# First loads in another order, weights in quarters, GpSimd left out of the front, and a scheduler with other durations

## The chip, the cores and the metric

The kernel runs on one core of one Trainium2 chip. The metric is the device time of one execution in microseconds, as the median of several runs. Beside the runs stands one execution that the hardware profiler recorded; every row shown here is from that one. Engines have the names of the profile: PE is TensorE's matmul, PEld its weight load, DVE is VectorE, ACT is ScalarE, POOL is GpSimd, SP issues the DMAs.

## What is computed

A decoder trunk of two layers on 512 tokens of width 2048, with 16 learned tokens in front (528 columns in all). Only the first step and the first products of layer 0 matter to the change; the rest is here so that the work behind them can be seen.

```
h = concat(meta_tokens, x)                 # 528 x 2048
h = layer_norm(h, ln_in_g, ln_in_b)
for l in range(2):
    proj = h @ w_in[l]                     # 2048 -> 5120, split in nine parts
    c = c_val * sigmoid(c_glu)             # convolution branch: 31 taps, norm, silu, product
    att = sliding_window_attention(q, k, v, sinks)
    r = rg_lru(causal_conv(r_x))           # recurrent branch
    mixed = concat(c', att', r') @ w_out[l]   # 2048 -> 2048, each branch gated by silu
    h = layer_norm(alpha * h + mixed, ln_post_g[l], ln_post_b[l])
return h[16:]
```

## The kernel before

Data lies with features on the partitions and the 528 tokens in columns. Each float32 product is made of three float32r matmuls: weights and activations are split into a high part (a copy that rounds to float32r) and a low part (the subtraction of it), and `mm3` sums high by high, high by low and low by high. The products of one tile of 128 output features run over 16 blocks of 128 input features.

**The front.** Five tiles of x (four of 128 tokens and one of 16, 2048 wide, loaded in four chunks of 512) come in as rows of tokens (`x_load`). `x_norm` takes statistics of each chunk on VectorE, the root on ScalarE and the reciprocal on VectorE, and scales the four chunks. `turn` transposes one block of 128 features on TensorE into PSUM, brings it out with the gains applied (ScalarE, to `e`), copies it to float32r (VectorE, the cast) and subtracts (GpSimd for three blocks in four, VectorE for the fourth). Phase 0 of the first products covers tiles 0 and 1 (256 columns), phase 1 tiles 2 to 4 (272 columns). In `gemms` the first three output tiles (glu 0, val 0, glu 1) run together, block by block, so that each block of h is used by nine matmuls of a phase as soon as `turn` has it: 144 matmuls in phase 0 and 144 in phase 1. From then on one output tile follows another, both halves of the columns at once.

**Weights.** `weight_load` brings pieces of 128 x 1024 (512 KB) into a ring of two raw buffers (`NRAW`); `weight_split` makes high parts on ScalarE and low parts on VectorE, 512 columns at a time, and frees the raw buffer. The first pieces are the first halves of three tiles, then their second halves.

**The order of the work.** Nothing is ordered by the hardware alone: `Sched` is a planner that runs while the program is built. Every thread (`k.spawn(prio, ...)`) yields one operation at a time with an engine and a reckoned duration; `run` takes the operation that could start first by its own clock, and of equals the one with the lower number. The program of each engine is the order that comes out, and each engine then keeps to it. SP's queue is one more engine ("Q") for the planner. Units ("u") are 78 buffers of one tile that weights, h and temporary results share; `Alloc` takes them by the planner's clock.

The reckoned durations that the change touches are in `mm`, `dma` and `_head`:

```
c = max(n / 2400, self._size(w) / 1200) + 0.003
return self._op("Q", max(0.45, n / 360e3), o, i, ..., 2.0)
kind = next((c for c in r.kinds if len(self.slots[c]) > (0 if r.weight or c != "u" else max(0, 10 - 2 * self.wheld))), None)
```

## Time and profile before

| what | value |
|---|---|
| median of 3 runs | 1490.77 us (1488.93 to 1490.9) |
| the profiled execution | 1489.76 us |
| its span, from first to last instruction | 1488.0 us |
| PE busy | 1451.8 us (98%) |
| VectorE busy | 1049.1 us (71%) |
| ScalarE busy | 706.3 us (47%) |
| GpSimd busy | 20.3 us (1%) |
| loaded and stored | 142.32 MB, mean 96 GB/s |

The profiled execution's own time is 1.76 us over its span and 1.01 us under the median of the runs. A share of busy time is an average over stages with other limits; PE is counted as busy from the start of a matmul to its modelled end, and matmuls overlap, so that short waits between them do not show in the 98%.

### The profile page before, as it was taken

The page shows a single profiled execution, that of the slowest core. Times are in us where ns is not written, and L with a number is a line of the kernel's source. Part 1 is how long each engine was busy: PE and PEld are TensorE (multiplying, and loading weights), DVE is VectorE, ACT ScalarE, POOL GpSimd, SP SyncE. Part 2 cuts the span into 40 slices and gives each one's busy share as a digit, 9 for nine tenths or more (in the row PEclk, how much of TensorE's full clock was granted, in tenths as well). Part 3 has the DMA queues.
Part 4 walks back from the last instruction along what each step waited for, and adds up shares of the span by engine and source line. Part 5 has one row for each costly group of instructions (what it writes and reads, how often), then busy time and mean ns, then how long its engine had stood idle before and what let it go on. Part 6 is the DMA issues. An engine that isn't in the chain of part 4 may idle for free.

```text
span 1488.0 us, 25171 instructions
## 1 busy us (share of the span) xinstructions
PE 1451.8 (98%) x10028; PEld 1350.8 (91%) x10028; DVE 1049.1 (71%) x2111; ACT 706.3 (47%) x1539; POOL 20.3 (1%) x28
## 2 busy tenths in 40 slices
PE   4999999999999999999999999999999999999996
PEld 3999999999999999999999997998788888888885
DVE  7798999984588443354688889999747864434437
ACT  5412458883377332222368134778735853323221
POOL 2200000000000000000000000000000000000000
PEclk9999999999999999999999999999999999999999
DMA  6312522243221223232433033223232222523323
GB/s 231 93 57 85 143 86 65 62 138 106 80 72 58 85 86 114 72 100 85 132 111 93 29 107 120 79 61 118 88 103 86 71 72 90 163 88 114 100 71 113
DMA packets 56549, 142.32 MB, mean 96 GB/s; under 512 B 12464, under 2 KB 20912, under 8 KB 56432
## 3 DMA queue, kind: packets, MB, share of 16 engines
q1 hardware_dynamic: 56432, 140.73, 30.8%
q8 instruction: 78, 1.28, 0.4%
q14 instruction: 39, 0.32, 0.1%
HBM read 128.12 MB, written 4.19 MB: 89 GB/s over the span
## 4 chain that ended last, share of the span: by engine, by line
PE 88%; DVE 7%; ACT 2%; DMA 1%; issue 1%; SPq 0%; DVEq 0%; ACTq 0%
PE p L184 68%; PE b L184 18%; DVE u L160 5%; PE b L188 2%; DVE a L160 2%; ACT u L174 1%; DMA w<-in_win 1%; DVE s L160 0%; DMA a<-in_x 0%; DVE t L160 0%; ACT t L174 0%; DVE P L160 0%; DMA u<-u 0%; SPq L194 0%; PE p L188 0%
## 5 line engine op out<-in xcount | busy, mean ns | idle before, releaser
L184 PE MATMUL p<-u,u 128*128 128x264 f32 (+3 forms) x7824 | 1181.4, 306 | 4.1 <-DVE u L160 2.9
L184 PEld LDWEIGHTS p<-u,u 128*128 128x128 f32 x7824 | 1064.5, 189 | 61.8 <-DVE u L160 4.6
L160 DVE TENSOR_TENSOR u<-w,u 128x512 fp32r<-128x512 f32 x456 | 306.0, 689 | 174.0 <-ACT u L174 170.6
L174 ACT ACTIVATE u<-w 128x512 fp32r<-128x512 f32 x456 | 273.0, 622 | 241.8 <-DMA w<-in_wout 124.3
L184 PE MATMUL b<-u,u 128*128 128x512 f32 (+6 forms) x1568 | 290.5, 324 | 4.3 <-DVE u L160 3.2
L184 PEld LDWEIGHTS b<-u,u 128*128 128x128 f32 (+2 forms) x1568 | 241.4, 185 | 33.9 <-DVE u L160 4.6
L160 DVE SCALAR_TENSOR_TENSOR a<-u,dp,a 128x527 f32<-128x527 f32 (+14 forms) x240 | 179.7, 749 | 4.2
L174 ACT ACTIVATE P<-P,s 100x257 f32<-100x257 f32 (+5 forms) x240 | 111.2, 479 | 28.7 <-DVE s L160 28.7
L160 DVE TENSOR_TENSOR u<-u,u 128x528 f32<-128x528 f32 (+5 forms) x146 | 100.8, 697 | 20.8 <-ACT u L174 17.9
L174 ACT ACTIVATE u<-p 128x528 f32<-128x528 f32 (+2 forms) x71 | 42.4, 598 | 149.0 <-PE p L184 148.8
L174 ACT ACTIVATE u<-u 64x528 fp32r<-64x528 f32 (+5 forms) x112 | 63.8, 584 | 81.0 <-DVE u L160 74.9
L160 DVE SCALAR_TENSOR_TENSOR u<-u,p 128x528 f32<-128x528 f32 (+3 forms) x45 | 30.7, 683 | 68.7 <-ACT u L174 50.6
L174 ACT ACTIVATE t<-b 128x400 fp32r<-128x400 f32 (+3 forms) x112 | 57.1, 510 | 44.0 <-PE b L184 22.0
L160 DVE CUSTOM_DVE_ANT_0 P<-b,con,nsink 100x256 f32<-100x256 f32 (+2 forms) x160 | 67.1, 450 | 3.1 <-PE b L184 2.2
L160 DVE TENSOR_TENSOR t<-b,t 128x400 fp32r<-128x400 f32 (+2 forms) x72 | 41.7, 579 | 13.4 <-ACT t L174 13.0
L184 PE MATMUL b<-t,u 128*128 128x400 f32 (+2 forms) x144 | 50.5, 351 | 0.0
L188 PE MATMUL b<-con,P 100*128 100x100 f32 (+2 forms) x320 | 44.1, 253 | 0.0
L174 ACT ACTIVATE u<-b 128x256 fp32r<-128x256 f32 (+4 forms) x28 | 11.8, 443 | 57.7 <-PE b L188 51.1
L188 PEld LDWEIGHTS b<-con,P 100*128 100x128 f32 (+2 forms) x320 | 35.9, 140 | 3.1 <-DVE s L160 0.4
L160 DVE TENSOR_SCALAR P<-P,s 100x256 f32<-100x256 f32 (+3 forms) x88 | 31.5, 363 | 0.7
L160 DVE SCALAR_TENSOR_TENSOR u<-u,u 128x528 f32<-128x528 f32 (+1 forms) x40 | 27.5, 699 | 5.2 <-ACT u L174 4.7
L174 ACT ACTIVATION_READ_ACCUMULATOR P<-P,s 100x1 f32 (+2 forms) x160 | 30.2, 189 | 0.0
(103 smaller groups left out, 656.7 us busy)
## 6 DMA issues: line engine op xcount, KB each, us to landing
w<-in_win SPq DMA_DIRECT2D x160, 512.0 KB, 3.7
w<-in_wout SPq DMA_DIRECT2D x64, 512.0 KB, 4.1
u<-u SPq DMA_DIRECT2D x48, 120.0 KB, 2.2
a<-in_x SPq DMA_DIRECT2D x8, 256.0 KB, 5.1
P<-in_x SPq DMA_DIRECT2D x8, 256.0 KB, 6.0
u<-u SPq DMA_DIRECT2D x16, 128.0 KB, 2.1
w<-in_pw SPq DMA_DIRECT2D x8, 256.0 KB, 2.6
out<-a SPq DMA_DIRECT2D x8, 256.0 KB, 2.3
```

The source lines that it names most:

```text
L160: return self._op("V", c, outs, ins, lambda: f(**kw))
L174: op = self._op("S", c, outs, ins, lambda: f(**kw))
L184: return self._op("T", c, [out], [w, x], lambda: f(out, w, x, start=start, stop=stop))
L188: return self._op("T", max(2 * self._size(ident) / 2400, 0.11) + 0.005, [out], [x, ident], lambda: f(out, x, ident))
```

## The change

It does these things, all of them in the planning program; what is computed stays the same.

- Loads: after x tile 0 comes the identity (now a tile of its own), then x tile 1 in two halves of 512 KB, then the gains and shifts of the first norm as a small tile of their own (`gin`). The first three weights come in quarters of 128 x 512 (256 KB) into units instead of the two raw buffers. `XBEFORE` and `WBEFORE` set the order: six quarters, tile 2, three quarters, tile 3, three quarters, tile 4, then the parameters and the constants.
- GpSimd has no work left in `turn`; the subtractions are VectorE's.
- A thread may yield a pair of operations; `_head` takes the one that would end first by the reckoned times, with 0.6 us added for VectorE. Scaling of chunks, the eviction in `turn`, the cast and the high parts of the early weights are such pairs of ScalarE and VectorE.
- `x_turn` starts the blocks of a chunk when that chunk is scaled in all tiles of the phase, not when whole tiles are. Low parts of the early weights wait until the first chunk of tile 1 is scaled (`go`). Four threads split the quarters, each with its own number.
- Durations: 0.445 ns a column and 4.5 ns for a matmul, 400 GB/s and 2.65 us of latency for a load.
- Evictions of PSUM (`E`) may take units down to four free ones instead of up to ten; `take_rx` frees the PSUM of the recurrent branch ahead of the wait in `recur`. The same edit from `U()` to `E()` in `values`, `conv_point` and `gate` is left out below.

```diff
+XBEFORE = (2, 2, 3, 4)
+WBEFORE = (0, 0, 6, 9, 12)
...
-    def __init__(self, kinds, dt=F32, w=L, weight=False):
-        self.kinds, self.dt, self.w, self.weight = kinds, dt, w, weight
+    def __init__(self, kinds, dt=F32, w=L, weight=False, keep=10):
+        self.kinds, self.dt, self.w, self.weight, self.keep = kinds, dt, w, weight, keep
...
-        self.free["Q"] = 0.8
+        self.free["Q"] = 0.75
...
-        c = max(n / 2400, self._size(w) / 1200) + 0.003
+        c = max(0.445e-3 * n, self._size(w) / 1200) + 0.0045
...
-        return self._op("Q", max(0.45, n / 360e3), o, i, lambda: f(out=out, in_=in_), 2.0)
+        return self._op("Q", max(0.45, n / 400e3), o, i, lambda: f(out=out, in_=in_), 2.65)
...
+            if isinstance(r, tuple):
+                return min(r, key=lambda o: self._start(o) + o.cost + (0.6 if o.eng == "V" else 0.0))
...
-                kind = next((c for c in r.kinds if len(self.slots[c]) > (0 if r.weight or c != "u" else max(0, 10 - 2 * self.wheld))), None)
+                kind = next((c for c in r.kinds if len(self.slots[c]) > (0 if r.weight or c != "u" else max(0, r.keep - 2 * self.wheld))), None)
...
-    con = cp.tile([128, NCONST], F32, name="con")
-    k.fixed = {par.tensor.name, con.tensor.name}
-    ident = con[:, C_ID:C_ID + 128]
+    con = cp.tile([128, C_ID], F32, name="con")
+    ident = cp.tile([128, 128], F32, name="ident")
+    gin = cp.tile([128, 32], F32, name="gin")
+    k.fixed = {par.tensor.name, con.tensor.name, gin.tensor.name, ident.tensor.name}
...
+    def E(keep=4):
+        return Alloc("u", F32, L, False, keep)
...
-    pieces = [(w, i) for i in range(2) for w in stream[0:NGROUP[0]]]
-    pieces += [(w, i) for w in stream[NGROUP[0]:] for i in range(-(-w.src.shape[1] // 1024))]
-    flow = dict(ahead=AHEAD, held=0, loaded=0)
+    pieces = [(w, 512 * i, 512) for i in range(4) for w in stream[0:NGROUP[0]]]
+    early = len(pieces)
+    pieces += [(w, i, min(1024, w.src.shape[1] - i)) for w in stream[NGROUP[0]:] for i in range(0, w.src.shape[1], 1024)]
+    flow = dict(ahead=AHEAD, held=0, loaded=0, x=0, split=0, go=False)
...
-        for w, i in pieces:
-            m = min(1024, w.src.shape[1] - 1024 * i)
-            raw = yield Alloc("w")
-            yield k.dma(raw[:, 0:m], w.src[:, 1024 * i:1024 * i + m])
-            w.raw.append((raw, m))
+        for n, (w, c, m) in enumerate(pieces):
+            if n < early:
+                yield Until(lambda: flow["x"] >= XBEFORE[n // NGROUP[0]])
+                raw = yield U(F32, 512)
+            else:
+                raw = yield Alloc("w")
+            yield k.dma(raw[:, 0:m], w.src[:, c:c + m])
+            w.raw.append((c, raw))
...
-    def weight_split():
-        for w, i in pieces:
-            yield Until(lambda: len(w.raw) > i)
-            raw, m = w.raw[i]
+    def weight_split(which):
+        for n in which:
+            w, c, m = pieces[n]
+            yield Until(lambda: w.raw and w.raw[-1][0] >= c and flow["split"] == n)
+            raw = next(r for o, r in w.raw if o == c)
...
-                yield S(out=wh, in_=r, func=AF.Copy)
+                a = S(out=wh, in_=r, func=AF.Copy)
+                yield (a, V("tensor_copy", out=wh, in_=r)) if n < early else a
+                yield Until(lambda: flow["go"])
...
+            flow["split"] += 1
...
-    xtok, xown = [None] * 5, [None] * 5
+    xtok, xown = [[None] * 4 for _ in range(5)], [None] * 5
...
-            own = []
+            yield Until(lambda: flow["loaded"] >= WBEFORE[i])
...
-                xt = [big[:, c, 0:512] for c in range(4)]
+                big = big.rearrange("p a c -> p (a c)")
+                xt = [big[:, 512 * c:512 * c + 512] for c in range(4)]
...
+                own = []
...
-            for c in range(4):
-                op = k.dma(xt[c][0:rows], t["x"][i * 128:i * 128 + rows, c * 512:(c + 1) * 512])
-                op.outs = [f"x{i}{c}"]
+            step = 2 if i == 1 else 1
+            for c in range(0, 4, step):
+                out = big[:, 512 * c:512 * (c + step)] if i < 2 else xt[c][0:rows]
+                op = k.dma(out, t["x"][i * 128:i * 128 + rows, c * 512:(c + step) * 512])
+                op.outs = [f"x{i}{c + s}" for s in range(step)]
+                if i == 1:
+                    op.lat += 1.0
...
-            k.spawn((0.8 if i < 2 else 1.42) + 0.01 * i, x_norm(i, xt, own))
-            if i == 4:
-                yield Until(lambda: flow["loaded"] >= 6)
-                yield k.dma(con[:, 0:C_ID], t["con"][:, 0:C_ID])
+            k.spawn((0.8 if i < 2 else 1.8) + 0.01 * i, x_norm(i, xt, own))
+            if i == 0:
+                yield k.dma(ident, t["con"][:, C_ID:NCONST])
...
-                yield k.dma(con[:, C_ID:NCONST], t["con"][:, C_ID:NCONST])
-                yield k.dma(par, t["par"])
-            if i in (1, 2):
-                yield Until(lambda: flow["loaded"] >= i)
+                yield k.dma(gin, t["par"][:, P_G0:P_G0 + 32])
+            flow["x"] = i + 1
+        yield k.dma(par, t["par"])
+        yield k.dma(con, t["con"][:, 0:C_ID])
...
+        def scale(c):
+            x = xt[c][0:rows]
+            ops = (V("tensor_scalar", out=x, in0=x, scalar1=mv[0:rows, 0:1], scalar2=mv[0:rows, 1:2], op0=ALU.subtract, op1=ALU.mult),
+                   S(out=x, in_=x, func=AF.Identity, scale=mv[0:rows, 1:2], bias=mv[0:rows, 2:3]))
+            for op in ops:
+                op.outs = [f"x{i}{c}"]
+                op.ins = [f"x{i}{c}", mv.tensor.name]
+            yield ops if c else ops[0]
+            xtok[i][c] = xt[c]
+        yield from scale(0)
+        if i == 1:
+            flow["go"] = True
...
-        for c, x in enumerate(xt):
-            x = x[0:rows]
-            if i > 1 or c > 2:
-                yield V("tensor_scalar", out=x, in0=x, scalar1=mv[0:rows, 1:2], scalar2=mv[0:rows, 2:3], op0=ALU.mult, op1=ALU.add)
-            else:
-                yield S(out=x, in_=x, func=AF.Identity, scale=mv[:, 1:2], bias=mv[:, 2:3])
+        for c in range(1, 4):
+            k.spawn((1.38 if i < 2 else 1.8) + 0.1 * c, scale(c))
+        yield Until(lambda: xtok[i][3] is not None and xtok[i][1] is not None and xtok[i][2] is not None)
...
-        xtok[i] = xt
...
-            for i in tiles:
-                yield Until(lambda: xtok[i] is not None)
...
-                k.spawn(1.4 + 0.2 * f, turn(f, d, tiles))
+                yield Until(lambda: all(xtok[i][d // 4] is not None for i in tiles))
+                k.spawn(1.85 if f else 1.4 + 0.1 * (d // 4), turn(f, d, tiles))
...
-            yield k.tr(ps[:, o:o + ROWS[i]], xtok[i][d // 4][0:ROWS[i], cs], ident[0:ROWS[i], 0:ROWS[i]])
+            op = k.tr(ps[:, o:o + ROWS[i]], xtok[i][d // 4][0:ROWS[i], cs], ident[0:ROWS[i], 0:ROWS[i]])
+            op.ins = [f"x{i}{d // 4}", ident.tensor.name] + ([x.tensor.name for x in xown[i]] if d == KT - 1 else [])
+            yield op
...
-        g, bb = par[:, P_G0 + d:P_G0 + d + 1], par[:, P_G0 + 16 + d:P_G0 + 17 + d]
+        g, bb = gin[:, d:d + 1], gin[:, 16 + d:17 + d]
...
-        yield S(out=e[:, 0:n], in_=ps[:, 0:n], func=AF.Identity, scale=g, bias=bb)
+        yield (S(out=e[:, 0:n], in_=ps[:, 0:n], func=AF.Identity, scale=g, bias=bb),
+               V("tensor_scalar", out=e[:, 0:n], in0=ps[:, 0:n], scalar1=g, scalar2=bb, op0=ALU.mult, op1=ALU.add))
...
-        yield V("tensor_copy", out=hi[:, c0:c0 + n], in_=e[:, 0:n])
-        yield (G if d % 4 < 3 else V)("tensor_tensor", out=lo[:, c0:c0 + n], in0=e[:, 0:n], in1=hi[:, c0:c0 + n].bitcast(F32), op=ALU.subtract)
+        yield (V("tensor_copy", out=hi[:, c0:c0 + n], in_=e[:, 0:n]), S(out=hi[:, c0:c0 + n], in_=e[:, 0:n], func=AF.Copy))
+        yield V("tensor_tensor", out=lo[:, c0:c0 + n], in0=e[:, 0:n], in1=hi[:, c0:c0 + n].bitcast(F32), op=ALU.subtract)
...
-        e = yield U()
+        e = yield E()
...
-        c = yield U()
+        c = yield E()
...
-        x = yield U()
-        s = yield U()
+        x = yield E()
...
+        s = yield U()
...
-    def recur(y, j, pr):
-        l, d = y.l, dp[y.l]
-        x = yield U()
+    def take_rx(y, j, pr):
+        x = yield E()
...
+        k.spawn(7, recur(y, j, x))
+    def recur(y, j, x):
+        l, d = y.l, dp[y.l]
...
-            k.spawn(2 if fn is not recur else 7, fn(y, i, pr))
+            k.spawn(2, fn(y, i, pr))
...
-        todo += [(recur, j, FULL) for j in range(4)]
+        todo += [(take_rx, j, FULL) for j in range(4)]
...
-        k.spawn(1, weight_split())
+        for q in range(4):
+            k.spawn(1.35 + 0.1 * q, weight_split(range(q * NGROUP[0], (q + 1) * NGROUP[0])))
+        k.spawn(1, weight_split(range(early, len(pieces))))
...

```

## Rows read from the trace of the kernel before

**Rows 1.** Costliest groups on PE, 76 to 1480 us: busy, mean | idle before.

```profile
L184 PE MATMUL p<-u,u 128*128 128x264 f32 (+1 forms) x7629 | 1145.6, 305 | 2.5 <-DVE u L160 1.6 <-ACT u L174 0.7
L184 PE MATMUL b<-u,u 128*128 128x264 f32 (+4 forms) x1472 | 272.0, 326 | 2.2 <-DVE u L160 1.2 <-ACT u L174 0.9
```

**Rows 2.** Chain that ended last, 0 to 90 us: start, length, what.

```profile
5.57 6.38 DMA w<-in_win
...
34.68 0.35 PE b L184 x3
...
35.74 0.36 PE b L184 x3
...
47.06 0.91 PE b L188 x6
...
51.10 0.38 PE b L188 x3
...
75.33 14.72 PE p L184 x119
```

**Rows 3.** Timeline of PE, 64 to 67 us: start, length, instructions.

```profile
64.73 0.93 PE L184 MATMUL p<-u,u 128*128 128x272 f32 x6
...
65.87 0.90 PE L184 MATMUL p<-u,u 128*128 128x272 f32 x6
```

**Rows 4.** Timeline of all engines, 9 to 19 us, from the second x tile on.

```profile
10.05 1.40 DVE L160 BATCH_NORM_STATS2 s<-a 128x6 f32<-128x512 f32 x2
...
11.04 0.69 PE L188 MATMUL b<-con,a 128*128 128x128 f32 x2 [11.04 <-ACT a L174]
...
11.48 0.26 DVE L160 BATCH_NORM_AGGREGATE s<-s 128x2 f32<-128x24 f32 x1
11.78 0.29 ACT L174 ACTIVATE s<-s,cst 128x1 f32<-128x1 f32 x1
...
12.11 0.16 DVE L160 RECIPROCAL s<-s 128x1 f32<-128x1 f32 x1 [0.36 <-ACT s L174]
...
15.84 0.54 ACT L174 ACTIVATE t<-b,par 128x256 f32<-128x256 f32 x1
...
18.45 0.58 PE L184 MATMUL p<-u,u 128*128 128x256 f32 x1 [1.32 <-DVE u L160]
```

**Rows 5.** Groups on VectorE and GpSimd, 10 to 62 us, each shape apart.

```profile
L160 DVE CAST u<-t 128x272 fp32r<-128x272 f32 x16 | 9.1, 571 | 4.8 <-ACT t L174 4.6
L160 DVE CAST u<-t 128x256 fp32r<-128x256 f32 x16 | 5.3, 353 | 0.9 <-ACT t L174 0.9
...
L160 DVE TENSOR_TENSOR u<-t,u 128x256 fp32r<-128x256 f32 x4 | 1.7, 413 | 0.0
...
L167 POOL TENSOR_TENSOR u<-t,u 128x256 fp32r<-128x256 f32 x12 | 10.4, 884 | 23.5 <-DVE u L160 23.5
L167 POOL TENSOR_TENSOR u<-t,u 128x272 fp32r<-128x272 f32 x12 | 9.7, 813 | 18.3 <-DVE u L160 18.3
```

**Rows 6.** Groups on ScalarE, 4 to 62 us, each shape apart.

```profile
L174 ACT ACTIVATE u<-w 128x512 fp32r<-128x512 f32 x16 | 9.8, 622 | 4.6 <-DMA w<-in_win 4.6
...
L174 ACT ACTIVATE t<-b,par 128x256 f32<-128x256 f32 x16 | 8.7, 559 | 5.7 <-PE b L188 5.5 <-POOL u L167 0.2
```

**Rows 7.** One line on VectorE, 19 to 62 us: duration ns min/median/max.

```profile
L160 DVE CAST u<-t x31: 270/302/869, 19.7 to 61.7; 128x272 fp32r<-128x272 f32 x16, 128x256 fp32r<-128x256 f32 x15
L160 DVE TENSOR_TENSOR u<-w,u x13: 657/679/1230, 19.0 to 61.0; 128x512 fp32r<-128x512 f32 x13
L160 DVE TENSOR_SCALAR P<-P,s x8: 521/535/973, 25.0 to 43.1; 128x512 f32<-128x512 f32 x8
```

**Rows 8.** Stretches: busy us of PE, PEld, DVE, ACT, POOL; clock; DMA; GB/s.

```profile
10.00:15.00 5.00, 1.38 (x4) 0.58 (x4) 3.44 (x10) 4.74 (x8) 0.00 (x0) 1.00 1.04 404
...
25.00:30.00 5.00, 2.88 (x13) 2.24 (x14) 5.00 (x11) 2.78 (x6) 2.70 (x3) 0.69 0.01 2
30.00:35.00 5.00, 5.00 (x31) 5.00 (x30) 4.14 (x11) 3.25 (x6) 2.84 (x3) 0.63 0.73 203
```

More of the change, by code (lines that the diff above doesn't have):

```diff
@@ L637, in conv_point @@
     def conv_point(y, j, pr):
-        o = yield U()
+        o = yield E()
         for pv, ov in pr.views(o):
@@ L684, in values @@
     def values(y, p, pr):
-        x = yield U()
-        m = yield U()
+        x = yield E()
         for pv, xv in pr.views(x):
@@ L689, in values @@
         pr.free()
+        m = yield U()
         mv = m[:, 0:384].rearrange("p (n c) -> p n c", n=3)
@@ L819, in recur_weights @@
             y.rw.append(p)
-    def recur(y, j, pr):
-        l, d = y.l, dp[y.l]
-        x = yield U()
+    def take_rx(y, j, pr):
+        x = yield E()
         for pv, xv in pr.views(x):
@@ L869, in gate @@
         a = pr.a
-        e = yield U()
+        e = yield E()
         for pv, ev in pr.views(e):
```

## The prediction

> **What bounds the kernel now.** I read three views in this order. The groups on TensorE behind 76 us come first: over 1404 us the two large groups waited 2.5 and 2.2 us in all [rows 1]. The reader should see that behind the front of the kernel there is next to nothing to win; the matmuls run back to back and their number does not change. So what the change is worth must come out of the first 75.33 us, where the chain of waits meets the first long run of matmuls (119 in 14.72 us, 0.124 us each) [rows 2].
>
> Second, the chain and the timeline inside the front give the pace of TensorE when nothing holds it. In phase 0 (256 columns) nine matmuls take 35.74 - 34.68 = 1.06 us [rows 2]; in phase 1 (272 columns) 65.87 - 64.73 = 1.14 us [rows 3]. The front has 16 such nines in each phase: 17.0 and 18.2 us. Three transposes of phase 1 take 0.38 us [rows 2], 16 times: 6.1. Phase 0 has 32 of 128 columns; two thirds of 0.38, 0.25 a pair, make 4.0. Sum 45.3 us of work. The first transpose starts at 11.04 [rows 4], so 75.33 - 11.04 - 45.3 = 19.0 us of the front are waits or slow clock.
>
> Third, where the 19.0 lie. Phase 0 should go at 45 matmuls in 5 us, and the stretches 25 to 30 and 30 to 35 hold 13 and 31 instructions on TensorE. Their granted clock is 0.69 and 0.63: worked out over two levels, 3.1 and 3.7 us at 1.2 GHz, after TensorE had been idle for 2.12 us of the first stretch [rows 8]. VectorE is busy for all of 25 to 30 [rows 8]. It is what feeds TensorE here: the first matmul waited for it until 18.45, 7.4 us behind the first transpose [rows 4].
>
> **The change part by part.**
>
> *Start.* Today tile 1 of x has its statistics at 11.45 and 11.74, its root at 11.78 and its reciprocal at 12.11 to 12.27 [rows 4]. The new order scales the first chunk at once on VectorE, 0.535 us [rows 7]: transposes at 12.8. Tile 1 now comes in two halves, so the last two statistics (1.40 us for two [rows 4]) can both start only when the second half is there, up to 0.7 later: 13.5. I take 13.1, since only the identity now goes ahead of tile 1. From there: transposes, an eviction of 0.559 [rows 6], a cast of about 0.28 [rows 7]; the first matmul comes near 14.5 instead of 18.45. Today the first eviction ran at 15.84, long after its transposes at 11.04 [rows 4], because ScalarE was scaling and splitting; these no longer queue ahead of it. I charge 1.0 us of TensorE's time for this chain.
>
> *GpSimd left out.* Its 24 subtractions (12 of 884 ns, 12 of 813 ns) go to VectorE, where the same shape takes 413 ns: 24 x 0.413 = 9.9 us more on an engine that is already full [rows 5]. Against that, VectorE's own work shrinks. A cast takes 270 ns at best, 302 in the middle and 869 at worst [rows 7], and the means are 353 and 571 ns [rows 5], the larger ones while GpSimd works. Brought to 280 and 302 ns, the 32 casts give back 16 x 0.073 + 16 x 0.269 = 5.5 us. The net load is 4.4 us. The Trainium skill (SBUF — State Buffer, Who interferes with whom) says that a GpSimd instruction and a VectorE cast or two-input operation lock a shared port against each other for a whole instruction; by that, the 5.5 us come back in full and the sum stands; if the stretched casts had another origin, the 5.5 would stay on VectorE and, shared by two engines, add 2.7 us of waits. The trace's 869 and 1230 ns speak for the lock.
>
> *Work to whichever engine is free.* The supply of phase 0 behind 13.1 us: 16 evictions x 0.559, 16 casts x 0.28, 16 subtractions x 0.413, 12 weight copies x 0.622, 12 weight subtractions x 0.68, three chunks x 0.535: 8.9 + 4.5 + 6.6 + 7.5 + 8.2 + 1.6 = 37.3 us [rows 5 to 7], 18.7 on each of two engines if it splits evenly. Statistics (8 x 0.70 [rows 4]) and scaling (8 x 0.535 [rows 7]) of tiles 2 and 3 add 9.9, or 4.9 each: 23.6. TensorE wants 17.0 + 4.0 + 2.7 (clock, below) = 23.7. They are level, so waits are between 0 and 5 us (all of tiles 2 and 3 in the way); I take 2.5. VectorE alone must do 6.6 + 8.2 + 5.6 = 20.4. The trace has no cast on ScalarE and no eviction on VectorE at this size; between the cast's 0.28 and the 512-column copy's 0.622 [rows 6] I count the former, and use the waits' upper end for the latter.
>
> *Clock.* TensorE at 1.2 GHz needed until inside 30 to 35 to come back, with the whole of that stretch busy [rows 8]. Starting from rest I allow 5.4 us at the lower level: 2.7 lost. The bounds are 0 and 6.8 us of half speed as found today, 3.4 lost.
>
> *Loads in quarters.* SP now issues x tile 0, the identity, x tile 1 and the gains, then six weight quarters of 256 KB, tile 2, three quarters, tile 3, three quarters, tile 4, par and con. The quarters have buffers of their own, so none waits for a split to free one of two. Tile 1 is there at 10.5 or so, when its last statistics run [rows 4]. At 404 GB/s [rows 8] a quarter of three weights (0.79 MB) takes 1.95 us: the first is there near 13. The last of the fourth comes 5.26 MB behind tile 1, 13.0 us, at about 23.5; it is wanted at the twelfth block, 14.5 + 12 x 1.31 = 30. I cost the loads at nothing; their cover is those 6 us. Par and con, moved to the end of the queue, are wanted only behind phase 1, since the gains of the first norm are now a small load of their own.
>
> *Phase 1.* Of the 19.0 us, 4.0 fall here: from its first transposes at 47.06 to 75.33 [rows 2] are 28.3 us, less 18.2 and 6.1. With evictions shared I take 2.0, bounds 0 and 4.
>
> *The scheduler's durations.* A 264-column matmul was reckoned at 0.113 us, is reckoned at 0.122 now, and runs at 0.124 [rows 2]. All orders behind the front are drawn up anew. The waits there are 4.7 us [rows 1]; I take 1.5 of them as gained, bounds 4.7 gained and 4.7 lost. Early release of PSUM (take_rx, conv_point, E) is part of this.
>
> **Sum.** 13.1 + 1.0 + 45.3 + 2.7 + 2.5 + 2.0 = 66.6 instead of 75.33: 8.7 us, and 1.5 behind it: 10.2. The profiled execution took 1489.76 us, so 1479.6; it lies 1.0 below the median of the runs, 1490.77, which makes **1480.6** by the median.
>
> **Rivals.** *VectorE stays the bound.* If casts and the scaling of tiles 2 and 3 go to it as well, it has 20.4 + 4.5 + 4.3 = 29.2 us, 5.5 over TensorE's 23.7; these come on top of the 2.5, and the time is 1486.1. For it: VectorE full from 25 to 30 [rows 8]. Against: the pick by finishing time moves casts away.
>
> *The quarters come late.* A weight DMA of today took 6.38 us in the chain [rows 2], and in 30 to 35 the queue moved 203 GB/s [rows 8]. At that rate 5.26 MB take 25.9 us, the last quarter is there at 36.4 instead of 30, and the time is 1487.0. It begins to matter under 5.26 MB in 19.5 us, 270 GB/s. Against: 256 KB pieces made up most of the 404 GB/s. The Trainium skill (DMA: Bandwidth & Descriptors, Bandwidth) says to batch transfers to 1 MiB or more for three quarters of the peak, which speaks against quarters; between its table's 64 KB and 1 MB an estimate of 250 GB/s would bring the last quarter at 31.5 and the time to 1482. The table was measured on another issuing path, and the trace's 404 disagrees.
>
> *The clock stays down: the other side.* If gaps in phase 0 keep TensorE at 1.2 GHz through phase 0's 21 us of work, this loses 18.3 more than my 2.7, less the 2.5 of waits that hide in it: 1496.4. It decides from 13.2 us more of lost work on, for 3 us slower. Against: at half speed TensorE needs 42 us where the supply needs 23.6, so the gaps close by themselves, and a busy stretch brought the clock back [rows 8].
>
> *The new orders behind the front go otherwise* by the bounds above: 1477.4 to 1486.8.
>
> **Chances.** Forecast 0.62, its own range 1475.8 to 1485.5 (waits 0 to 5, phase 1 0 to 4, start 12.8 to 13.5). VectorE 0.17, late quarters 0.06, clock 0.04, new orders 0.11. The range takes in the better end of the new orders with no waits, 1474, and the late quarters, 1488. What this kernel's measurement can tell is about 0.2%, 3 us. Faster: forecast, VectorE, four fifths of the new orders and a little of the quarters, 0.88. Same 0.07; slower 0.05, the clock and the worst orders.
>
> **What would show it.** GpSimd has no work behind 1 us; casts stay near 0.30 us; the first matmul stands at 14 to 15; phase 0 ends near 39 and the first long run of matmuls starts at 64 to 69; one spell of half clock instead of a second one; behind it TensorE's waits stay under 5 us. I am wrong if a weight DMA ends a wait of TensorE's suppliers in phase 0, if half clock lasts past 20 us, or if waits behind the front grow over 5 us.

## The result, and the profile after

The changed kernel is slower. It takes 1506.55 us (median of 6 runs, 1501.44 to 1510.11) where the kernel before, on the same chip, takes 1490.35: a ratio of 1.0108, with an interval of 1.0088 to 1.0129. The profiled execution took 1504.39 us, its span is 1502.6. The forecast was 1480.6, and the range ended at 1488.

The first lines to read are those that answer to [rows 2], the chain up to 90 us (start, length, what).

```profile
40.43 1.13 PE b L191 x6
...
69.67 20.45 PE p L187 x166
```

The front did what it should, in part: the long run of products starts at 69.67 instead of 75.33. That is 5.7 us gained of the 8.7 foreseen. So some 20 us went lost behind it, where the prediction had 1.5 to gain. The groups on TensorE from 76 to 1470 us, beside [rows 1], show only a part of that: 3.0 and 7.6 us of waits for 2.5 and 2.2. (L187 is the helper that makes the products, L191 the transposes, L163 VectorE's operations, L177 ScalarE's; in the kernel before they stand at L184, L188, L160 and L174.)

```profile
L187 PE MATMUL p<-u,u 128*128 128x264 f32 (+1 forms) x7583 | 1139.5, 306 | 3.0 <-ACT u L177 2.3 <-DVE u L163 0.7
L187 PE MATMUL b<-u,u 128*128 128x264 f32 (+3 forms) x1381 | 255.5, 325 | 7.6 <-DVE u L163 6.0 <-issue 0.8 <-ACT u L177 0.6
```

Matmuls overlap and their ends are modelled, so a stall of a few tenths hides in the busy time. What TensorE gets through in the same stretch shows more of it: the number of its instructions, and the busy time of its weight loads (PEld, the second pair of figures). Here are four stretches of the kernel before (columns as in [rows 8]):

```profile
76.00:200.00 124.00, 123.52 (x1018) 123.34 (x1017) 114.48 (x200) 37.28 (x75) 0.00 (x0) 1.00 0.31 91
200.00:290.00 90.00, 90.00 (x741) 89.40 (x739) 85.68 (x214) 72.72 (x193) 0.00 (x0) 1.00 0.24 70
290.00:860.00 570.00, 568.09 (x4639) 565.80 (x4638) 367.64 (x702) 257.24 (x529) 0.00 (x0) 1.00 0.29 90
860.00:985.00 125.00, 124.59 (x854) 115.34 (x853) 117.43 (x257) 69.64 (x183) 0.00 (x0) 1.00 0.32 98
```

And the same four of the kernel after:

```profile
76.00:200.00 124.00, 121.67 (x996) 120.84 (x995) 120.25 (x203) 37.16 (x75) 0.00 (x0) 1.00 0.31 90
200.00:290.00 90.00, 87.76 (x691) 84.50 (x690) 82.33 (x206) 74.72 (x194) 0.00 (x0) 1.00 0.21 62
290.00:860.00 570.00, 567.02 (x4614) 562.78 (x4613) 357.55 (x689) 252.51 (x522) 0.00 (x0) 1.00 0.29 89
860.00:985.00 125.00, 122.40 (x808) 111.16 (x807) 120.58 (x255) 62.36 (x164) 0.00 (x0) 0.99 0.34 100
```

TensorE does 22, 50, 25 and 46 instructions less. At the pace of before in each stretch (124 / 1018 us and so on) that is 2.7 + 6.1 + 3.1 + 6.7 = 18.6 us, an estimate, since the same stretch need not hold the same mix of instructions in both. The busy time of the weight loads falls by 2.5, 4.9, 3.0 and 4.2 us. The loss sits in 200 to 290 and 860 to 985 above all; at 860 to 985 VectorE is busy for 117 to 121 of 125 us in either kernel. Followed matmul by matmul (how much sooner the n-th matmul of 264 columns starts than in the kernel before, which has as many), the lead is 5.7 us at 76 and 3.6 at 200. It turns into a lag of 3.8 by 280, which is 6.0 at 700, 6.3 at 860 and 15.2 at 985; at the end the spans differ by 14.6.

The second thing to read is the front, in the timeline from the first transposes to the first product (start, length, instructions, idle time before and what ended it), beside [rows 4].

```profile
9.40 0.69 PE L191 MATMUL b<-ident,a 128*128 128x128 f32 x2 [9.40 <-DVE a L163]
...
13.95 0.69 PE L191 MATMUL b<-ident,a 128*128 128x128 f32 x2 [3.86 <-DMA u<-in_win]
...
15.08 0.54 DVE L163 TENSOR_SCALAR t<-b,gin 128x256 f32<-128x256 f32 x1
...
15.68 0.71 ACT L177 ACTIVATE u<-t 128x256 fp32r<-128x256 f32 x2
...
16.45 0.58 PE L187 MATMUL p<-u,u 128*128 128x256 f32 x1
```

The first matmul starts at 16.45, not 18.45. Then TensorE does not wait until the end of phase 0. Its clock is at the lower level until 19.0 us and full from there to 42.9. The timeline of weight loads shows the change, three in 0.76 us and then six in 0.79:

```profile
18.14 0.76 PEld L187 LDWEIGHTS p<-u,u 128*128 128x128 f32 x3
...
19.24 0.79 PEld L187 LDWEIGHTS p<-u,u 128*128 128x128 f32 x6
```

Single matmuls of 256 columns take 415 ns up to 18.6 us and some 280 from 19.0 on; in the stretch 30 to 35 us of the kernel before, which has both levels [rows 8], they take the same two times. The first record of the clock stands at 19.0 us in this trace and at 23.5 in that of the kernel before. For what lies ahead of it the view of stretches shows 1.00, as in the row 10 to 15 of [rows 8], and that is no reading of the clock.

At the start of phase 1 TensorE does wait, as the timeline shows from 34 to 41 us.

```profile
34.42 0.29 ACT L177 ACTIVATE s<-s,cst 128x1 f32<-128x1 f32 x1
...
36.45 0.82 ACT L177 ACTIVATE P<-P,s 128x512 f32<-128x512 f32 x1 [1.25 <-DVE s L163]
...
37.59 0.60 PE L191 MATMUL b<-ident,P 128*128 128x128 f32 x4
...
39.06 0.29 PE L191 MATMUL b<-ident,u 16*128 16x16 f32 x2 [0.87 <-DVE u L163]
...
40.43 0.44 PE L191 MATMUL b<-ident,P 128*128 128x128 f32 x2 [1.09 <-ACT t L177]
```

The root of tile 2 runs at 34.42, though its statistics were there at 22.33. In the code, the norm of tiles 2 to 4 has number 1.8. The quarters and the blocks of phase 0 have 1.35 to 1.7, the split of the later weights has 1, so all of these go ahead of it on two engines that are full (the stretch 30 to 35 below: VectorE 5.00 us, ScalarE 5.00). The later weights' part in this is two operations on each of the two, 1.3 us, from 32.63 on. Tiles 2 to 4 are scaled only when TensorE already wants them, and the gaps of 0.87 and 1.09 us follow. Behind them the clock falls:

```profile
30.00:35.00 5.00, 5.00 (x45) 5.00 (x44) 5.00 (x12) 5.00 (x14) 0.00 (x0) 1.00 0.35 140
35.00:40.00 5.00, 3.48 (x30) 3.15 (x28) 4.98 (x16) 3.51 (x8) 0.00 (x0) 1.00 0.35 105
40.00:45.00 5.00, 4.57 (x23) 3.61 (x23) 1.90 (x5) 4.72 (x12) 0.00 (x0) 0.79 0.00 0
45.00:50.00 5.00, 5.00 (x21) 3.75 (x20) 1.27 (x4) 2.04 (x5) 0.00 (x0) 0.53 0.01 3
50.00:55.00 5.00, 5.00 (x33) 4.18 (x33) 3.33 (x8) 4.75 (x12) 0.00 (x0) 1.00 0.00 0
```

Over two levels, 0.79 and 0.53 are 2.1 and 4.7 us at 1.2 GHz, 6.8 in all, so some 3.4 us are lost. In 45 to 50 TensorE is busy without a break and does 21 instructions, where 50 to 55 has 33.

### The profile page after: what moved, and what is told of

It reads as the page before. It is cut to its first block, busy times and chain, and to the rows that moved or that the text cites. A ratio compares the mean times of both kernels' runs of the same rounds, so it can differ in the third digit from the quotient of the medians.

```text
span 1502.6 us, 25186 instructions
## 1 busy us (share of the span) xinstructions
PE 1463.2 (97%) x10028; PEld 1352.5 (90%) x10028; DVE 1042.6 (69%) x2102; ACT 715.9 (48%) x1572; POOL 0.2 (0%) x4
## 4 chain that ended last, share of the span: by engine, by line
PE 80%; DVE 11%; ACT 4%; DMA 3%; issue 2%; SPq 1%; DVEq 0%; ACTq 0%
PE p L187 61%; PE b L187 16%; DVE u L163 7%; DVE a L163 3%; ACT u L177 3%; PE b L191 2%; DVE P L163 1%; DMA u<-in_win 1%; DMA w<-in_win 1%; SPq L197 1%; ACT L177 0%; ACT t L177 0%; DMA u<-u 0%; DVE t L163 0%; ACT P L177 0%
## 5 line engine op out<-in xcount | busy, mean ns | idle before, releaser
L187 PE MATMUL p<-u,u 128*128 128x264 f32 (+3 forms) x7824 | 1180.0, 306 | 3.0 <-ACT u L177 2.3
L187 PEld LDWEIGHTS p<-u,u 128*128 128x128 f32 x7824 | 1064.1, 189 | 60.3 <-ACT u L177 3.2
L163 DVE TENSOR_TENSOR u<-w,u 128x512 fp32r<-128x512 f32 x444 | 295.7, 687 | 177.7 <-ACT u L177 176.3
L177 ACT ACTIVATE u<-w 128x512 fp32r<-128x512 f32 x444 | 264.2, 622 | 246.1 <-DMA w<-in_wout 114.9
L187 PE MATMUL b<-u,u 128*128 128x512 f32 (+6 forms) x1568 | 295.6, 327 | 7.6 <-DVE u L163 6.0
L187 PEld LDWEIGHTS b<-u,u 128*128 128x128 f32 (+2 forms) x1568 | 240.5, 185 | 42.9 <-DVE u L163 10.5
L163 DVE SCALAR_TENSOR_TENSOR a<-u,dp,a 128x527 f32<-128x527 f32 (+14 forms) x240 | 179.7, 750 | 4.9 <-ACT a L177 0.2
L177 ACT ACTIVATE P<-P,s 100x257 f32<-100x257 f32 (+6 forms) x243 | 113.5, 484 | 36.2 <-DVE s L163 36.0
L163 DVE TENSOR_TENSOR u<-u,u 128x528 f32<-128x528 f32 (+5 forms) x158 | 108.8, 696 | 20.1 <-ACT u L177 17.9
L177 ACT ACTIVATE u<-p 128x528 f32<-128x528 f32 (+2 forms) x71 | 42.4, 598 | 158.8 <-PE p L187 158.6
L177 ACT ACTIVATE u<-u 128x512 fp32r<-128x512 f32 (+5 forms) x124 | 71.6, 589 | 97.0 <-DVE u L163 90.4
L163 DVE SCALAR_TENSOR_TENSOR u<-u,p 128x528 f32<-128x528 f32 (+3 forms) x45 | 30.8, 684 | 76.6 <-ACT u L177 63.4
L177 ACT ACTIVATE t<-b 128x400 fp32r<-128x400 f32 (+3 forms) x112 | 57.0, 509 | 31.2 <-PE b L187 17.3
L163 DVE CUSTOM_DVE_ANT_0 P<-b,con,nsink 100x256 f32<-100x256 f32 (+2 forms) x160 | 66.7, 451 | 1.0 <-PE b L187 0.7
L187 PE MATMUL b<-t,u 128*128 128x400 f32 (+2 forms) x144 | 53.6, 372 | 0.5 <-DVE t L163 0.3
L163 DVE TENSOR_TENSOR t<-b,t 128x400 fp32r<-128x400 f32 (+2 forms) x72 | 41.6, 578 | 14.8 <-ACT t L177 14.5
L191 PE MATMUL b<-ident,P 100*128 100x100 f32 (+2 forms) x320 | 45.4, 258 | 1.1 <-ACT t L177 1.1
L177 ACT ACTIVATE u<-b 128x256 fp32r<-128x256 f32 (+4 forms) x28 | 11.8, 445 | 60.4 <-PE b L191 52.9
L191 PEld LDWEIGHTS b<-ident,P 100*128 100x128 f32 (+2 forms) x320 | 36.0, 142 | 4.9 <-DVE s L163 1.3
L163 DVE TENSOR_TENSOR u<-t,u 128x264 fp32r<-128x264 f32 (+2 forms) x64 | 26.3, 426 | 10.5 <-ACT u L177 10.5
L187 PEld LDWEIGHTS b<-t,u 128*128 128x128 f32 x144 | 27.0, 187 | 6.1 <-ACT t L177 1.7
L177 ACT ACTIVATION_READ_ACCUMULATOR P<-P,s 100x1 f32 (+2 forms) x160 | 30.3, 189 | 0.0
```

What stands on the lines that cost most here:

```text
L163: return self._op("V", c, outs, ins, lambda: f(**kw))
L177: op = self._op("S", c, outs, ins, lambda: f(**kw))
L187: return self._op("T", c, [out], [w, x], lambda: f(out, w, x, start=start, stop=stop))
L191: return self._op("T", max(2 * self._size(ident) / 2400, 0.11) + 0.005, [out], [x, ident], lambda: f(out, x, ident))
```

## The experiments

Each kernel was timed against the kernel before on the same chip, whose median was 1489.84 to 1490.0. The ratio is that of the means.

| kernel | median (runs), us | lowest to highest | ratio to before | interval |
|---|---|---|---|---|
| mm_back | 1486.43 (10) | 1484.68 to 1494.65 | 0.9989 | 0.9971 to 1.0007 |
| dma_back | 1509.2 (4) | 1508.22 to 1509.29 | 1.0125 | 1.011 to 1.014 |
| evict_back | 1516.71 (4) | 1510.0 to 1518.56 | 1.0165 | 1.0138 to 1.0193 |
| front_alone | 1494.59 (10) | 1489.01 to 1499.91 | 1.0029 | 1.0011 to 1.0047 |
| before_true_mm | 1516.13 (4) | 1513.5 to 1516.84 | 1.0168 | 1.0151 to 1.0185 |
| lag_reckoned | 1486.55 (7) | 1483.0 to 1493.18 | 0.9983 | 0.9963 to 1.0004 |
| filled | 1486.23 (7) | 1485.9 to 1487.89 | 0.9975 | 0.9964 to 0.9986 |
| pool_back | 1483.16 (4) | 1482.39 to 1484.6 | 0.9953 | 0.9939 to 0.9968 |
| pool_half_margin | 1490.24 (10) | 1488.53 to 1492.49 | 1.0004 | 0.9994 to 1.0013 |
| pool_more_margin | 1498.77 (4) | 1498.38 to 1500.22 | 1.006 | 1.0045 to 1.0075 |
| before_evict | 1489.39 (10) | 1488.54 to 1491.14 | 0.9997 | 0.9988 to 1.0007 |
| pool_late_split | 1481.35 (4) | 1481.04 to 1482.11 | 0.9942 | 0.9927 to 0.9957 |

**Which of the edits behind the front.** Three edits reach beyond the front: the matmul's reckoned duration, the load's, and the early evictions with their smaller reserve of units. Each was undone alone, and then all three.

mm_back, from after:

```
-        c = max(0.445e-3 * n, self._size(w) / 1200) + 0.0045
+        c = max(n / 2400, self._size(w) / 1200) + 0.003
```

> The changed kernel with one edit undone: the scheduler reckons a matmul as before (columns/2400 + 0.003 us, 0.113 us for 264 columns, where the chip takes 0.124). Theory M (margin): the too short matmul of before made the scheduler put whatever waits for VectorE and ScalarE later among the products than needed, and that hid their lags; with the true duration the margin is gone and TensorE waits for them (171, 237, 300, 910, 1045 us). Then this run keeps the 5.7 us won in the front and loses the 20 behind it: 1484 to 1489. Theory E (evictions): the waits come from the units and the PSUM being taken earlier (E, take_rx); this run stays near 1506. Theory D (loads): they come from the loads' new reckoning; this run stays near 1506. Theory S (shift): any new front shifts the rest and spoils it; near 1500 to 1506.

dma_back, from after:

```
-        self.free["Q"] = 0.75
+        self.free["Q"] = 0.8
...
-        return self._op("Q", max(0.45, n / 400e3), o, i, lambda: f(out=out, in_=in_), 2.65)
+        return self._op("Q", max(0.45, n / 360e3), o, i, lambda: f(out=out, in_=in_), 2.0)
```

> The changed kernel with the scheduler's reckoning of loads as before (360 GB/s, 2.0 us of latency, queue free at 0.8). Theory D: 1484 to 1492. Theories M, E and S: within 4 us of the changed kernel's 1506.

evict_back, from after (take_rx becomes a part of recur again):

```
-    def E(keep=4):
+    def E(keep=10):
...
-        todo += [(take_rx, j, FULL) for j in range(4)]
+        todo += [(recur, j, FULL) for j in range(4)]
```

> The changed kernel with the evictions as before: units down to ten free ones, the recurrent branch's product brought out and held by recur itself. Theory E: 1484 to 1492. Theories M, D and S: within 4 us of 1506.

front_alone is after with all three of these edits undone.

> The changed kernel with all three undone (matmul and load reckoning, evictions), so that only the front is new: order of loads, quarters, no GpSimd, work to the free engine. Theories M, E and D: the front's gain alone, 5.7 us: 1483 to 1487. Theory S: near 1500.

One line decides: with the old reckoning of the matmul the time falls from 1506.55 to 1486.43. In the stretches above, mm_back does 727 instead of 691 instructions, and 850 instead of 808:

```profile
200.00:290.00 90.00, 88.91 (x727) 87.86 (x726) 83.23 (x205) 72.43 (x190) 0.00 (x0) 1.00 0.20 64
...
860.00:985.00 125.00, 124.19 (x850) 114.91 (x849) 118.83 (x262) 71.05 (x189) 0.00 (x0) 1.00 0.33 99
```

dma_back gives nothing back: 1509.2, with an interval that overlaps that of after; behind the front it loses 17.7 us where after loses 20.3. evict_back is 10 us slower than after by the medians, which neither of its expectations had. Between the profiled executions it is 12.4; matmul by matmul, 6.6 of these stand in the front and 5.8 behind it. The front of both, and of front_alone, met a longer spell at half clock, so front_alone missed its expectation: 1494.59. Its stretches, columns as before:

```profile
40.00:45.00 5.00, 4.16 (x20) 3.19 (x21) 1.98 (x5) 4.54 (x12) 0.00 (x0) 0.78 0.00 0
45.00:50.00 5.00, 5.00 (x22) 4.20 (x20) 1.59 (x4) 2.38 (x6) 0.00 (x0) 0.50 0.01 3
50.00:55.00 5.00, 5.00 (x20) 3.75 (x18) 0.79 (x2) 2.51 (x6) 0.00 (x0) 0.50 0.00 0
55.00:60.00 5.00, 5.00 (x20) 4.10 (x20) 3.32 (x7) 3.83 (x9) 0.00 (x0) 0.50 0.26 69
60.00:65.00 5.00, 5.00 (x26) 4.45 (x26) 0.54 (x2) 1.34 (x4) 0.00 (x0) 0.67 0.09 36
```

At 1.2 GHz the profiled execution spent 2.2 + 15 + 3.3 = 20.5 us, TensorE busy for 5.00 of 5 from 45 us on; some 10.2 us are lost, and the gain of the front with them (its long run starts at 75.77). In dma_back the spell is 23.9 us, in mm_back 3.4. It also varies for one kernel: of the ten runs of mm_back, the three at 1494.46 to 1494.65 are those whose mean clock is 0.989 or 0.99, the others (1484.68 to 1488.19) have 0.995 to 0.997. This makes its interval wide, and it means that what the evictions or the loads do in the front is not told apart from the length of the spell here.

**Why a truer duration costs time.** The theory after these runs: the planner compares engines. A 264-column matmul reckoned at 0.113 us instead of the measured time (0.124 in the chain of [rows 2], 0.122 from one start to the next in the trace of after) let TensorE look fast, so that the planner put more of other products ahead of a matmul that needs the result of VectorE and ScalarE. What those two really take beyond their reckoning would be covered by that (more on this below). At 0.122 the cover is gone, and TensorE, which keeps to its order, waits. The rival: the new orders are worse by chance, or by something else in the change. Two kernels tell them apart. before_true_mm is the kernel before with the matmul's line of the change and nothing else:

```
-        c = max(n / 2400, self._size(w) / 1200) + 0.003
+        c = max(0.445e-3 * n, self._size(w) / 1200) + 0.0045
```

> The kernel before with one edit alone: matmuls reckoned at 0.445 ns a column and 4.5 ns. Theory M: slower than before by 10 to 25 us, 1500 to 1515, all of it behind 130 us. If the loss needs the new front: 1488 to 1493.

lag_reckoned is after, with the truer matmul, and VectorE's and ScalarE's reckoned durations 8% longer (in `V` and in `S`):

```
+        c *= 1.08
```

> The changed kernel, matmuls reckoned at their true 0.122 us, but every operation of VectorE and ScalarE reckoned 8% longer. Theory M (the margin between TensorE and its suppliers is what counts, not the matmul's own figure): as good as the run with the short matmul, 1484 to 1495. If the figure of the matmul itself is what matters (through weights and loads, which follow TensorE): near 1506.

The one line costs the kernel before 26 us (1516.13, 1 us over what was expected), and in the two stretches it does 678 and 813 instructions, as after does. With the other two engines reckoned 8% longer the truer matmul does no harm: 1486.55, 733 and 855.

```profile
200.00:290.00 90.00, 87.32 (x678) 84.34 (x677) 85.95 (x211) 72.51 (x190) 0.00 (x0) 0.98 0.20 62
860.00:985.00 125.00, 122.41 (x813) 111.88 (x812) 120.06 (x239) 56.84 (x145) 0.00 (x0) 0.99 0.32 100
```

The fence above is before_true_mm, the one below lag_reckoned.

```profile
200.00:290.00 90.00, 89.41 (x733) 88.56 (x732) 87.61 (x215) 72.99 (x192) 0.00 (x0) 1.00 0.22 68
860.00:985.00 125.00, 124.75 (x855) 115.38 (x854) 118.96 (x260) 70.85 (x186) 0.00 (x0) 1.00 0.33 100
```

So what counts here is the ratio between the engines' reckoned times, not the matmul's figure by itself. The rival of bad luck would have to explain four orders with the truer matmul alone (after, dma_back, evict_back, before_true_mm), all of which lose 18 to 26 us behind the front, and five with the old ratio, or a like one (mm_back, lag_reckoned and, told below, filled, pool_back, pool_late_split), that lose 3.0 at most. front_alone stands between with 7.2, lost in one place near 280 us, where its clock falls once more; so an unlucky order can come with the old ratio, too. A part of the loss is slow clock again: 3.4 us at 1.2 GHz from 913 us on in after, and three such spells behind the front in before_true_mm.

One part of the theory the traces do not bear out, that VectorE and ScalarE take longer than reckoned. In after, from one start to the next where they run back to back, VectorE's subtraction of 512 columns takes 602 ns (reckoned 598) and a tap of the convolution 668 (663), ScalarE's copy of 512 columns 522 (518). Of the operations compared only the scan of the recurrent branch is far off, 1168 for 615, and there are eight of them. So in after all three engines are reckoned close to what they take, and the order loses 20 us behind the front; in lag_reckoned the two suppliers are reckoned some 8% too long, and it loses nothing there. What the margin has to cover was not found.

What one such wait looks like is seen at the first matmul of the scores; in after's order of TensorE it stands behind 824 matmuls of 264 columns, in before's behind 829, in mm_back's behind 840. The timeline of weight loads, first after's, then mm_back's:

```profile
172.48 0.30 PEld L187 LDWEIGHTS b<-u,u 128*128 128x128 f32 x2 [1.68 <-DVE u L163]
```

```profile
172.48 0.30 PEld L187 LDWEIGHTS b<-u,u 128*128 128x128 f32 x2 [0.79 <-ACT P L177]
```

Both start at 172.48, when what it needs is there, but mm_back has put 16 more products before it, nine of them because its long run began 1.1 us sooner. In after the weight load waits 1.68 us, in mm_back 0.79. In the four kernels with the truer matmul alone this wait is 1.68 to 2.07 us, in the ten others 0.08 to 1.02.

**The gap at 38 us, and GpSimd.** Two causes were on the table for the front's 3.0 us that did not come: the gap with its spell of slow clock, and VectorE and ScalarE overloaded for lack of GpSimd. filled is mm_back with 24 products that nothing needs, as filler for TensorE between the last block of phase 0 and the last of phase 1:

```
+            yield k.mm(ps[:, 0:256], h[:, 0:128], h[:, 0:256], True, True)
...
+        k.spawn(9, fill(24))
```

> The changed kernel with the short matmul, and 24 spare matmuls of 256 columns, read by nobody, that TensorE may run while it has nothing else between phase 0 and the end of phase 1. They add no result. Theory C (the gap at 37 to 41 us lets the clock fall, and what it costs differs from run to run): clock 1.00 from 40 to 65 us, 1481 to 1485 and a spread under 4 us instead of 10. If the spell has another cause: spread and median stay (1486, up to 1494).

pool_back is mm_back with GpSimd's three subtractions in four:

```
-        yield V("tensor_tensor", out=lo[:, c0:c0 + n], in0=e[:, 0:n], in1=hi[:, c0:c0 + n].bitcast(F32), op=ALU.subtract)
+        yield (G if d % 4 < 3 else V)("tensor_tensor", out=lo[:, c0:c0 + n], in0=e[:, 0:n], in1=hi[:, c0:c0 + n].bitcast(F32), op=ALU.subtract)
```

> The changed kernel with the short matmul, and GpSimd doing three of four subtractions of the front again. If supply by VectorE and ScalarE is what opens the gap of TensorE at 37 to 41 us (theory L, load): the gap closes, the clock stays up, 1479 to 1484 with no run near 1494. If the shared port eats what GpSimd takes over (theory P): casts of 0.5 us again, the gap stays, 1485 or more.

The first fence is filled, the second pool_back, in stretches of 5 us.

```profile
40.00:45.00 5.00, 4.94 (x33) 3.78 (x32) 1.79 (x5) 4.10 (x10) 0.00 (x0) 1.00 0.01 3
45.00:50.00 5.00, 5.00 (x35) 4.06 (x33) 1.96 (x6) 4.31 (x11) 0.00 (x0) 1.00 0.00 0
```

```profile
40.00:45.00 5.00, 4.57 (x28) 3.25 (x28) 3.05 (x5) 4.56 (x11) 4.52 (x5) 1.00 0.01 3
45.00:50.00 5.00, 5.00 (x34) 4.22 (x34) 1.32 (x2) 4.31 (x10) 2.48 (x4) 1.00 0.00 0
```

Without the gap there is no spell: the clock is 1.00, and the runs of filled lie within 2 us where those of mm_back spread over 10. Its median is no better and misses what was expected; the 24 spare matmuls take some 2.8 us themselves, an estimate at 0.118 us each. pool_back, idle for 0.43 us in 40 to 45, has no spell either, and it gains: 1483.16, its long run starts at 66.79. GpSimd's price is there nonetheless. The groups of pool_back from 10 to 62 us:

```profile
L163 DVE TENSOR_TENSOR u<-t,u 128x272 fp32r<-128x272 f32 x4 | 3.6, 894 | 4.1 <-ACT u L177 4.1
...
L163 DVE TENSOR_TENSOR u<-t,u 128x256 fp32r<-128x256 f32 x4 | 2.4, 610 | 0.1
...
L170 POOL TENSOR_TENSOR u<-t,u 128x272 fp32r<-128x272 f32 x12 | 10.9, 925 | 8.4 <-ACT u L177 8.3
```

The same subtraction takes VectorE 894 and 610 ns here, and 438 and 413 in after, where GpSimd has no work (below). It is stretched, but 24 subtractions off VectorE are worth more. The Trainium skill (SBUF — State Buffer, Who interferes with whom) has the two engines lock each other out for a whole instruction when VectorE reads two operands from SBUF; the 894 ns agree with that.

**How much margin.** pool_half_margin and pool_more_margin are pool_back with a 264-column matmul reckoned at 0.118 and 0.101 us:

```
-        c = max(n / 2400, self._size(w) / 1200) + 0.003
+        c = max(n / 2300, self._size(w) / 1200) + 0.003
```

(n / 2700 in the second.)

> The run with GpSimd back, and a 264-column matmul reckoned at 0.118 us: half way between the short 0.113 and the true 0.122. Theory M in its simple form (the loss grows as the margin shrinks): between 1483 and the 1500 or so that the true duration would give, 1486 to 1495. If only an exact balance hurts: 1482 to 1485.

> The run with GpSimd back, and a 264-column matmul reckoned at 0.101 us. Theory M: waits behind the front go on shrinking, 1480 to 1483, unless operations now stand too late among the products and the end of a layer waits for them: 1485 or more.

Both are slower than pool_back's 1483.16 at 0.113. With half the margin the lead of 10.1 us at 76 is 4.9 at 280 and 1.3 at the end. With more margin a lead of 9.0 us grows to 10.2 by 740, is 5.5 at 860, behind 6.8 us at half clock from 757 on, and 7.2 at 985; then one wait turns it into a lag of 9. Its waits on TensorE from 1040 to 1100 us (what waited for what: us in total, times, longest), and the stretches:

```profile
PE p L187 <- ACT u L177: 13.1, 1, 13.1
```

```profile
1075.00:1080.00 5.00, 0.00 (x0) 0.00 (x0) 4.93 (x8) 2.45 (x4) 0.00 (x0) 0.80 0.02 10
1080.00:1085.00 5.00, 0.00 (x0) 0.00 (x0) 2.93 (x5) 1.94 (x3) 0.00 (x0) 0.50 0.00 0
```

TensorE runs out of other products and stands still for 13.1 us. So margin is not simply good; of the values tried, 0.113 is the best. Each value stands for one order alone, and this last one loses 18 us behind the front with no truer matmul, so the size of a loss does not by itself tell its cause.

**The evictions in the old front, and the gap's cause.** before_evict is the kernel before with the early release (`E`, take_rx) alone:

```
-        x = yield U()
+        x = yield E()
```

> The kernel before with one edit alone: evictions may take units down to four, and the recurrent branch's product leaves PSUM at once. If the edit is worth what undoing it cost in the new front (8 us by the medians, 4 by the best runs): 1482 to 1487. If it only mended what the new front had spoiled: 1489 to 1491.

pool_late_split is pool_back with the split of the later weights behind the norm of tiles 2 to 4:

```
-        k.spawn(1, weight_split(range(early, len(pieces))))
+        k.spawn(1.9, weight_split(range(early, len(pieces))))
```

> The run with GpSimd back, and the splitting of weights that are wanted only behind the front put behind the work of both phases (priority 1.9 instead of 1). If supply still holds TensorE in phase 1: another 1 to 2 us, 1481 to 1482.5. If not: 1482.5 to 1484.

The early release alone changes nothing that can be measured: 0.9997, 0.9988 to 1.0007. The later split brings the time to 1481.35, the best here, and faster than both kernels. TensorE is busy for all of 40 to 45, and the long run starts at 65.53.

```profile
40.00:45.00 5.00, 5.00 (x35) 4.13 (x34) 2.12 (x4) 4.50 (x11) 4.32 (x6) 1.00 0.25 95
```

## Why the prediction was wrong

**What bounds the kernel.** "Behind the front there is next to nothing to win" was right, and the wrong thing to read from it was that there is little to lose. [Rows 1] show what the order of before left over, 4.7 us; they say nothing of an order drawn up anew.

**The step that failed: the scheduler's durations.** It took 1.5 us as gained, with bounds of 4.7 either way, the lower one simply mirrored. Measured: 20.3 us lost behind the front (before_true_mm 26, mm_back 20.1 given back); the other two parts of the term, the loads' durations and the early release, gave nothing back when they were undone. Its own sign, waits behind the front over 5 us, came: 3.0 + 7.6. The prediction held 0.122 against the 0.124 of [rows 2], saw that it was truer, and did not ask what the 0.009 too little had been good for.

**Start.** It was to give the first matmul at 14.5; it came at 16.45. The transposes of tile 1 start at 13.95, not 13.1, since four of its statistics ran one behind another, and not two. The first eviction, on VectorE, then starts at 15.08, the cast at 15.68: VectorE subtracted and ScalarE split weights until then. That these "no longer queue ahead" was wrong. The 1.0 charged for the chain was right: TensorE waits 1.04 us for this eviction, from 14.64 to 15.67.

**Clock and waits in phase 0.** The clock's term (2.7) was needed, at about its size: from 13.95 to 19.0 TensorE is at the lower level, 1.04 us of it idle, so some 4 us of work and 2.0 lost. The prediction had found slow clock in the kernel before in 25 to 35 alone; that kernel, too, was at the lower level from its start, to 23.5. The waits (2.5) did not come. Phase 0 ends near 37.5, where the terms of the sum make 40.3 and 39 was named; this paid for part of what the start and phase 1 cost more.

**GpSimd left out.** The port's part was right: VectorE's subtractions take 413 and 438 ns. That casts would "move away" was right as well; all 32 went to ScalarE, at 410 and 418 ns rather than 0.28 us. The groups of after from 10 to 62 us, first VectorE, then ScalarE, beside [rows 5]:

```profile
L163 DVE TENSOR_TENSOR u<-t,u 128x272 fp32r<-128x272 f32 x16 | 6.4, 438 | 10.3 <-ACT u L177 10.3
L163 DVE TENSOR_TENSOR u<-t,u 128x256 fp32r<-128x256 f32 x16 | 6.2, 413 | 0.2 <-ACT u L177 0.2
```

```profile
L177 ACT ACTIVATE u<-t 128x272 fp32r<-128x272 f32 x16 | 6.0, 418 | 0.0
L177 ACT ACTIVATE u<-t 128x256 fp32r<-128x256 f32 x16 | 6.0, 410 | 0.0
```

But both engines were full to 35 us, and what was pushed back was tiles 2 to 4. The supply was summed for phase 0 and shared out evenly; the split of the later weights, which the change leaves ahead of the norm, was not in the sum. The net effect of leaving GpSimd out is a loss: 1486.43 us without GpSimd (mm_back), 1483.16 with it back (pool_back).

**Loads in quarters.** Right: no matmul of phase 0 waited for them, though one copy on ScalarE, at 11.89 and ahead of the phase, waited 0.93 us for the first quarter. They moved 378, 313, 336 and 298 GB/s in the four stretches from 10 to 30 us. This is far over the 250 GB/s that was estimated from the Trainium skill (DMA: Bandwidth & Descriptors, Bandwidth).

**Phase 1.** 2.0 us of waits were allowed (bounds 0 and 4). From 37.5 to 69.67 are 32.2 us, 7.9 over the work of 24.3: the two waits of the gap, 2.0, slow clock, 3.4, and 2.5 that no row tells apart. The rival "the clock stays down" had the mechanism, in phase 0 and not where it came; its "against", that a busy stretch brings the clock back, failed in front_alone for 20 us.

**The rival of new orders** had the right place and the wrong size: it ended at 1486.8. pool_late_split comes within 1 us of the time forecast for the change (1481.35), but it is another kernel, with the old matmul, GpSimd back and the later split, and does not bear the sum out.

## What to carry over

The durations in a planner that orders several engines are a set: to make one of them true can take away a margin that the engine fed by the others lived on, and a queue that keeps to its order then waits. So time such an edit alone, and look at the ratio it changes; here 8% on the feeding engines did as well as the old figure, and still more margin on the matmul cost time again. "The stage has no waits left" bounds a gain there, never a loss. When work moves between engines that feed a matmul stream, add up what the next phase needs of the same engines, too: a gap of 3 us cost up to 10 by the clock here.

## What the runs showed of the hardware

The clock fell to 1.2 GHz after a gap of some 3 us with short runs in it, and did not come back at once though TensorE was busy for all of the time: 3.4 us in mm_back, 6.8 in after, 20.5 in front_alone, 23.9 in dma_back. It goes with a spread of 10 us in the time of one and the same kernel. The Trainium skill (TensorE: Matmul & The Clock Gate, What's actually happening) says that the number of slow matmuls at the start of one and the same kernel varies from run to run; the ten runs of mm_back, with mean clocks of 0.989 to 0.997, show the like behind a gap. What decides between 3 and 24 us was not tried. With the gap filled or closed (filled, pool_back, pool_late_split) the spell did not come in the front of any of the three profiles, and the mean clock of all their 15 runs is 0.997 or 0.998.

TensorE starts at the lower level, too: until 19.0 us in after, 23.5 in before and 35.2 in before_true_mm, though in each it had matmuls to do from 16 to 19 us on.

A cast to float32r of 256 columns takes ScalarE 410 ns, of 272 columns 418, where [rows 7] have 270 at best on VectorE.
